# Moving the streamed operands of the matmuls to other start addresses, by pads and column offsets

## The chip, the cores and the metric

The kernel runs on one core of one Trainium2 chip. The metric is the device time of one execution in microseconds. Three runs of the kernel before gave 2610.64, 2612.74 and 2614.07 us; the median, 2612.74 us, is the time before.

## The reference

The model is a backbone of four layers over 256 context tokens and 256 latent tokens of width 1024. Each layer has a token mixer and a squared-ReLU MLP, each behind a modulated RMSNorm and a gated residual. Layers 0 and 3 mix with a bidirectional gated DeltaNet, layer 1 with a short gated convolution, layer 2 with differential attention.

```python
for i in range(DEPTH):
    h_lat = modulate(rmsnorm(x, norm1_g[i]), sh1, sc1)
    h_ctx = modulate(rmsnorm(x_ctx, norm1_g[i]), csh1, csc1)
    y_ctx, y_lat = mixer(h_ctx, h_lat, ...)          # z = h @ w_in; ...; y @ w_out
    x = x + g1 * y_lat
    x = x + g2 * mlp_sqrelu(modulate(rmsnorm(x, norm2_g[i]), sh2, sc2), mlp_w1[i], mlp_w2[i])
    if not last:
        x_ctx = ...                                   # the same for the context tokens
return rmsnorm(x, final_g)

def mlp_sqrelu(h, w1, w2):
    return jnp.square(jax.nn.relu(h @ w1)) @ w2       # 1024 -> 4096 -> 1024
```

All of it is float32. In the last layer only the latent tokens go on after the mixer.

## The kernel before

Activations lie feature-major: 128 features on the partitions, tokens along a row. A full row has TT = 512 columns, 256 context tokens and then 256 latent ones. A large product takes a weight block of 128 x 128 as the stationary operand of TensorE and streams 512 columns (both kinds of token) or 256 (one kind) past it.

To keep float32 accuracy, both operands are split into two parts in the format fp32r, and three matmuls are accumulated for each block (`prod`): weight-high with activation-high, weight-high with activation-low, weight-low with activation-high. The tiles are called `whi` and `wlo` (for the last weights of a stage `whix`, `wlox`) on the weights' side. On the activations' side they are `hh`, `hl` (the normalised input of a mixer or of an MLP), `u` (the squared hidden units of the MLP, high and low under one name in the profile), `y` (the mixer's output in DeltaNet and in attention; in DeltaNet's last heads it lies in tiles called `NT`) and `yh`, `yl` (the mixer's output in the convolution). Each matmul is its own weight load followed by its stream; the load of the next block runs while the present block streams.

Weights come by DMA on SP's queue into three `raw` tiles of 512 KB, ScalarE casts each into `whi`, VectorE (in DeltaNet often GpSimd) makes `wlo`; there are four pairs of `whi` and `wlo`.

A recording layer (`Issue`) takes operations from generators and writes them out by a table of assumed costs. So each engine's order is fixed at build time, and tile pools hand out addresses in the order in which tags are first asked for.

An MLP (`mlp`) takes eight steps. A step makes four blocks of hidden units from `hh`, `hl` (4 blocks x 8 chunks x 3 = 96 matmuls) and then the part of the output that comes from four `u` pairs (8 blocks x 4 x 3 = 96 matmuls). In layers 0 to 2 nearly all have 512 columns; the first step's joint part and the last output rounds are done in halves of 256 (`joint`, `proj_rounds`). In layer 3 the whole MLP has 256 columns, the latent ones, which are the right half of each 512-wide tile.

An address here is the byte offset in a partition, from the built program. The **distance** of a pair of matmuls is the start of the weight block that is being loaded minus the start of the columns that stream at that time, modulo 512. For example: `whi` starts at 54144 and `hh0` at 87680, so the distance is -33536 mod 512 = 256. All weight blocks of 128 columns start at 384 mod 512 (the `x` ones at 256), so the distance depends on the streamed tile alone.

Of the kernel before, what the change touches and what calls it, by code (L numbers as in the profile page):

```python
# [10 lines left out]
F32 = mybir.dt.float32  # L11
# [363 lines left out]
class Net:  # L375
# [3 lines left out]
    MM = 3  # L379
    HP, DHP = -20, -20  # L380
    SHARE = 0.7
    RAW = 3
    RINGS = (dict(u=4, kt=2, E=2, qd=1, NT=2, scr=2, Z=3, gate=2, o=3, NY=1),
             dict(u=4, kt=3, E=3, qd=3, NT=3, scr=3, Z=4, gate=4, o=4, NY=1))

    def __init__(self, tc, ctx, a, depth=4):
        self.tc, self.nc, self.ctx, self.a, self.depth = tc, tc.nc, ctx, a, depth
        self.I = Issue(tc.nc)
        pool = lambda name, bufs, **k: ctx.enter_context(tc.tile_pool(name=name, bufs=bufs, **k))
        self.cp = pool("cp", 1)  # L390
        self.wp = pool("wp", 1)
        self.sp = pool("sp", 1)
        self.psp = pool("psp", 1, space=PSUM)
        self.wlist, self.wt, self.wsplit, self.wraw, self.wdone = [], {}, 0, 0, -1
        self.whome, self.wheld, self.wpool = [], deque(), None
        self.mods = {}
        self.spare_dve = 0
        self.joined = False
        self.wide = True

    def const(self, name, shape, dt=F32):
        return self.I.tile(self.cp, name, shape, dt)
# [304 lines left out]
    def norm_strand(self, i, which, st, half, h):  # L707

        I = self.I
        yield from self.norm_rs(st, half)  # L710
        rs, r, c = st["rs"][half], 1 - half, HALF[half]
        if "A" not in st:
            st["A"] = I.tile(self.sp, f"gain{which}", [P, NCH, 2])
            st["Ak"] = set()
        A = st["A"]
        late = None
        for k in range(NCH):
            q = 12 * which + k // 2
            evs = [self.ada_ev[i][q], self.ada_ev[i][q + 4]]
            if late and not all(e.on for e in evs):  # L720
                yield I.stt(*late)
                I.rel(late[1])
                late = None
            yield evs + [self.tmp_slot(half)]
            mod = self.mods[i]
            if k // 2 not in st["Ak"]:
                st["Ak"].add(k // 2)
                yield from self.gain(i, which, A, k - k % 2)
            tmp = self.norm_tmp(half)
            yield I.stt(tmp, self.x[k][:, c], A[:, k, r:r + 1], rs, ALU.mult, ALU.mult)  # L730
            B = mod[:, 24 * which + k, r:r + 1]
            yield I.act(h[0][k][:, c], tmp, AF.Identity, bias=B)
            if late:
                yield I.stt(*late)
                I.rel(late[1])
            late = (h[1][k][:, c], tmp, B, h[0][k][:, c].bitcast(F32), ALU.add, ALU.subtract)
        yield I.stt(*late)
        I.rel(late[1])
        st["hev"][half].on = True

    def norm_start(self, i, which, st, halves=(0, 1)):
        I = self.I
        h = ([], [])
        for k in range(NCH):
            h[0].append(I.tile(self.sp, f"hh{k}", [P, TT], F32R))
            h[1].append(I.tile(self.sp, f"hl{k}", [P, TT], F32R))
        st["hev"] = [Event(), Event()]
        st["h"] = h
        for half in halves:
            I.spawn(self.norm_strand(i, which, st, half, h), 3 + half)  # L750


    def prod(self, ps, ah, al, bh, bl, first, last):
# [5 lines left out]
    def block(self, wn, rhs, kc, cols, ps, s=slice(0, P), m=P, off=0):  # L759


        c = slice(cols.start - off, cols.stop - off)
        yield [self.have(wn)]
        wh, wl = self.wt[wn]
        for k in range(kc):
            yield [wh, wl, rhs[0][k][:, c], rhs[1][k][:, c]]
            yield from self.prod(ps[0:m, cols], wh[:, k, s], wl[:, k, s], rhs[0][k][:, c], rhs[1][k][:, c], k == 0, k == kc - 1)

    def joint(self, wns, rhs, parts=HALF):


        group = []
        self.wide = False
        for n, wn in enumerate(wns):
            yield [self.mm_slot() if n >= len(wns) - self.MM else self.ch_slot()]
            group.append((wn, self.mm_ps() if n >= len(wns) - self.MM else self.ch_ps()))
        self.wide = True
        for c in parts:
            for k in range(NCH - self.LATE if c is parts[-1] else NCH):
                for wn, ps in group:  # L780
                    yield from self.joint_prod(wn, ps, rhs, c, k)
        return group, rhs, parts[-1]

    def joint_prod(self, wn, ps, rhs, c, k):
        yield [self.have(wn)]
        wh, wl = self.wt[wn]
        m = wh.shape[-1]
        yield [wh, wl, rhs[0][k][:, c], rhs[1][k][:, c]]
        yield from self.prod(ps[0:m, c], wh[:, k, :], wl[:, k, :], rhs[0][k][:, c], rhs[1][k][:, c], k == 0, k == NCH - 1)

    def joint_end(self, group, rhs, c, fin):

        for n, (wn, ps) in enumerate(group):
            for k in range(NCH - self.LATE, NCH):
                yield from self.joint_prod(wn, ps, rhs, c, k)
            self.done(wn)
            fin(n, ps)
            self.joined = n < len(group) - 1
# [53 lines left out]
    def mlp(self, i, t0, st, nst, pl):  # L852
        I = self.I
        halves = [h for h in range(2) if h * T >= t0]
        cols = self.full(t0)
        h = st["h"]
        first = yield from self.joint(pl[0, 0], h, [HALF[x] for x in halves])
        with self.tc.tile_pool(name=f"mlp{i}", bufs=1) as up:
            us = {}
            self.wpool = up  # L860
            ada = Event(i + 1 == self.depth)
            if not ada.on:
                I.spawn(self.ada_rows(i + 1, up, ada), 5000)

            def u_tiles(f):
                us[f] = tuple([I.tile(up, f"u{x}{m}", [P, TT], F32R, 2) for m in range(4)] for x in range(2))

            def u_fin(f, m, ps):
                yield [lambda: I.slot(up, "r", 2)]
                r = I.tile(up, "r", [P, TT], F32, 2, True)  # L870
                u = I.tile(up, "u", [P, TT], F32, 2, True)
                yield I.act(r[:, cols], ps[:, cols], AF.Relu)
                I.rel(ps)
                yield I.act(us[f][0][m][:, cols], r[:, cols], AF.Square)
                yield I.act(u[:, cols], r[:, cols], AF.Square)
                yield I.vtt(us[f][1][m][:, cols], u[:, cols], us[f][0][m][:, cols].bitcast(F32), ALU.subtract)
                I.rel(r, u)

            nf = FF // 512
            for f in range(nf):  # L880
                u_tiles(f)
                if f == 0:
                    yield from self.joint_end(*first, lambda m, ps: I.spawn(u_fin(0, m, ps), 2))
                for m in range(0 if f else 4, 4):
                    yield [self.mm_slot()]
                    ps = self.mm_ps()
                    yield from self.block(pl[0, f][m], h, NCH, cols, ps)
                    self.done(pl[0, f][m])
                    I.spawn(u_fin(f, m, ps), 2)
                if f:  # L890
                    yield from self.proj_rounds(i, pl[1, f - 1], 4, 2, us.pop(f - 1), t0, 40, None)
            if i + 1 < self.depth:
                self.norm_start(i + 1, 0, nst)
            yield from self.proj_rounds(i, pl[1, nf - 1], 4, 2, us.pop(nf - 1), t0, 40, nst)
            self.wpool = None
            yield [ada]

# [90 lines left out]
    def gdn_mixer(self, i, j, last, st, nst, pl):  # L988
# [6 lines left out]
        with self.tc.tile_pool(name=f"gd{i}", bufs=1) as gp:  # L995
# [15 lines left out]
            for step, s in enumerate(self.ORDER[j]):  # L1011
# [27 lines left out]
                else:  # L1039
# [1 line left out]
                    final = heads[-1] == H - 1  # L1041
                    yield [self.y_ev[m] for m in heads]
                    if final:
                        self.norm_start(i, 1, nst, (1,) if t0 else (0, 1))
                    y = [sum((list(self.y[m // 2][x]) for m in heads[::2]), []) for x in range(2)]
                    yield from self.proj_rounds(i, pl[s], len(y[0]), 8 // len(y[0]), y, t0, 16, nst if final else None, t0)
                    self.round_done[n].on = True
# [275 lines left out]
    def gated(self, n, o):  # L1323
# [8 lines left out]
        if last:  # L1332

            yield [self.made[H - 1], self.free("NT", 2)] if 3 not in self.y else []
            if 3 not in self.y:
                y = [self.take("NT", [P, 2, TT], F32R) for x in range(2)]
                self.y[3] = [[y[x][:, m, :TT - t0] for m in range(2)] for x in range(2)]
        elif n // 2 not in self.y:
            self.y[n // 2] = tuple([I.tile(self.gp, f"y{x}{m}", [P, TT - t0], F32R, self.NY) for m in range(2)] for x in range(2))
        yh, yl = self.y[n // 2]  # L1340
        yield from self.split_into(yh[n % 2], yl[n % 2], o)
# [207 lines left out]
    def diff_head(self, n, qk, evs):  # L1549
# [37 lines left out]
        yield I.stt(sq, po, self.gl, sq, ALU.mult, ALU.mult)  # L1587
        I.rel(po)
        if n // 4 not in self.y:
            self.y[n // 4] = tuple([I.tile(dp, f"y{x}{m}", [P, TT], F32R, self.NYD) for m in range(4)] for x in range(2))  # L1590
        yh, yl = self.y[n // 4]
        yield from self.split_into(yh[n % 4], yl[n % 4], sq)
# [194 lines left out]
```

## Time and profile before

| | |
|---|---|
| median of three runs | 2612.74 us |
| the profiled execution | 2613.07 us, with a span of 2611.4 us from first to last instruction |
| TensorE busy | 2515.1 us, 96% of the span |
| VectorE, ScalarE, GpSimd busy | 1899.4, 1257.6, 389.3 us |
| granted TensorE clock, mean | 0.987 |

Matmuls are pipelined, and the profile gives one a duration that reaches past the start of the next. So a matmul's price in a dense stream is the spacing from start to start, which is read from a window's length and the number of matmuls in it, and not the mean duration. Where a stretch has several lines of work, a window over one tile's matmuls counts those alone; a matmul that began just before the window is counted too.

### The profile page before, as it was taken

To read this page: it belongs to the slowest core of one execution; us is meant where nothing else is said; L and a number is where in the kernel's file an instruction comes from. 1 tells how busy PE (TensorE), PEld (TensorE's weight loads), DVE (VectorE), ACT (ScalarE), POOL (GpSimd) and SP (SyncE) were. 2 spreads that over 40 slices of the span, in tenths; PEclk is the share of its full clock that TensorE was granted. 3 is DMA by queue.
4 is the path that set the end of the run, shared out by engine and by line. 5 is a ranking of instruction groups with operands and counts; after the bars stand their busy time and mean duration, and the time that the engine had idled before them with its cause. 6 is when DMAs were issued, how large, how long until landed. Compare 5 with 4: busy or idle time off the path is not lost. (4 is left out here: it accounts for less than half of the span.)

```text
span 2611.4 us, 41997 instructions
## 1 busy us (share of the span) xinstructions
PE 2515.1 (96%) x16396; PEld 2091.5 (80%) x16396; DVE 1899.4 (73%) x3499; ACT 1257.6 (48%) x2343; POOL 389.3 (15%) x273
## 2 busy tenths in 40 slices
PE   6999999899999999999999999999999999997998
PEld 3677777788888988888889666888888878786998
DVE  5776677699975645899856767799965787776665
ACT  4565565543333423533343544543333677765554
POOL 0444444200000000000000000000000254454000
PEclk9999999999999999999999999999999999998999
DMA  6312212456544133565532222365633111122564
GB/s 264 119 50 73 90 50 74 154 189 213 196 144 129 59 97 104 187 210 200 169 115 77 64 73 66 114 213 199 210 124 111 49 50 50 50 58 81 163 185 130
DMA packets 91638, 323.30 MB, mean 124 GB/s; under 512 B 10288, under 2 KB 13872, under 8 KB 91056
## 3 DMA queue, kind: packets, MB, share of 16 engines
q1 hardware_dynamic: 91440, 320.62, 37.8%
q8 instruction: 129, 2.11, 0.3%
q14 instruction: 69, 0.57, 0.1%
HBM read 317.44 MB, written 1.05 MB: 122 GB/s over the span
## 5 line engine op out<-in xcount | busy, mean ns | idle before, releaser
L241 ACT CAST whi<-raw 128x1024 fp32r<-128x1024 f32 x380 | 399.0, 1050 | 799.7 <-PE ch L221 431.9
L254 DVE TENSOR_TENSOR wlo<-raw,whi 128x1024 fp32r<-128x1024 f32 x305 | 374.2, 1227 | 236.6 <-ACT whi L241 236.3
L221 PE MATMUL mm<-hh,whi 128*128 128x512 f32 (+1 forms) x1344 | 490.2, 365 | 1.8 <-DVE x L257 1.1
L221 PE MATMUL mm<-hh,wlo 128*128 128x512 f32 (+1 forms) x1344 | 489.9, 364 | 0.8 <-DVE wlo L254 0.8
L221 PE MATMUL mm<-hl,whi 128*128 128x512 f32 (+1 forms) x1344 | 488.7, 364 | 0.0
L261 DVE CUSTOM_DVE_ANT_0 adaj<-adat,adas,pack 128x1024 bf16<-128x1024 f32 x288 | 368.5, 1280 | 8.5 <-ACT adas L237 5.7
L221 PE MATMUL ch<-hl,whi 128*128 128x512 f32 (+3 forms) x784 | 281.8, 359 | 5.9 <-DVE hl L257 5.9
L221 PE MATMUL ch<-u,whi 128*128 128x512 f32 (+1 forms) x1024 | 287.4, 367 | 0.0
L221 PEld LDWEIGHTS mm<-hh,whi 128*128 128x128 f32 x1344 | 257.8, 192 | 34.4 <-issue 7.7
L221 PEld LDWEIGHTS mm<-hh,wlo 128*128 128x128 f32 x1344 | 257.7, 192 | 32.8 <-issue 6.5
L221 PE MATMUL ch<-hh,whi 128*128 128x512 f32 (+3 forms) x784 | 281.5, 359 | 2.1 <-ACT hh L237 2.1
L221 PE MATMUL ch<-hh,wlo 128*128 128x512 f32 (+3 forms) x784 | 282.1, 360 | 0.0
L221 PEld LDWEIGHTS mm<-hl,whi 128*128 128x128 f32 x1344 | 257.8, 192 | 29.4 <-issue 4.7
L280 POOL TENSOR_TENSOR wlo<-raw,whi 128x1024 fp32r<-128x1024 f32 x75 | 182.0, 2429 | 284.5 <-ACT whi L241 279.6
L221 PE MATMUL mm<-u,whi 128*128 128x512 f32 (+1 forms) x768 | 215.6, 367 | 0.0
L221 PEld LDWEIGHTS ch<-u,whi 128*128 128x128 f32 x1024 | 183.6, 188 | 34.8
L221 PEld LDWEIGHTS <-Z 128*128 128x128 f16 x3072 | 141.0, 98 | 86.2 <-issue 50.2
L221 PE MATMUL ch<-u,wlo 128*128 128x512 f32 (+1 forms) x512 | 187.9, 367 | 0.0
L280 POOL TENSOR_TENSOR qk<-qk,rope 128x512 f32<-128x512 f32 x8 | 13.5, 1685 | 1104.2 <-DMA rt<-qk 1100.4
L221 PE MATMUL ch<-Z 128*128 128x64 f16 (+1 forms) x2816 | 173.0, 201 | 4.8 <-DVE Z L248 3.4
L257 DVE SCALAR_TENSOR_TENSOR x<-mm,mod,x 128x256 f32<-128x256 f32 x285 | 129.4, 479 | 63.7 <-PE mm L221 63.7
L251 DVE CAST_PREDICATED Z<-lev,ch 128x256 f16<-128x256 uint8 x384 | 143.2, 426 | 42.5 <-PE ch L221 40.6
(257 smaller groups left out, 4614.5 us busy)
## 6 DMA issues: line engine op xcount, KB each, us to landing
raw<-in_mlp_w SPq DMA_DIRECT2D x256, 512.0 KB, 3.6
adat<-in_ada_wT SPq DMA_DIRECT2D x144, 512.0 KB, 4.5
raw<-in_gdn_w_in SPq DMA_DIRECT2D x64, 512.0 KB, 3.7
adaw<-in_ada_w SPq DMA_DIRECT2D x48, 512.0 KB, 4.9
raw<-in_sconv_w_in SPq DMA_DIRECT2D x24, 512.0 KB, 3.6
raw<-in_diff_w_in SPq DMA_DIRECT2D x24, 512.0 KB, 3.7
raw<-in_gdn_w_out SPq DMA_DIRECT2D x16, 512.0 KB, 3.6
raw<-in_sconv_w_out SPq DMA_DIRECT2D x8, 512.0 KB, 3.5
```

Of the source, the lines that this page charges most:

```text
L221: op = Op("PE", c, [out], [lhsT, rhs], lambda: self.nc.tensor.matmul(out, lhsT=lhsT, rhs=rhs, start=start, stop=stop, **k), LAT["PE"])
L241: lambda: self.nc.scalar.copy(out=out, in_=in_), LAT["ACT"])
L251: return self.vec(self._n(data), 68, [out], [data], lambda: self.nc.vector.copy_predicated(out=out, mask=mask, data=data))
L254: return self.vec(self._n(in0), 68, [out], [in0, in1], lambda: self.nc.vector.tensor_tensor(out=out, in0=in0, in1=in1, op=op))
L257: return self.vec(self._n(in0), 130, [out], [in0, in1, scalar], lambda: self.nc.vector.scalar_tensor_tensor(out=out, in0=in0, scalar=scala ...
L261: return self.vec(self._n(in0), 130, [out, junk], [in0, in1, init], lambda: self.nc.vector.tensor_tensor_reduce(out=junk, in0=in0, in1=in1 ...
L280: lambda: self.nc.gpsimd.tensor_tensor(out=out, in0=in0, in1=in1, op=op))
```

## The change

Tiles are moved; nothing else is. A dummy tile of 8 columns x n (32 n bytes) is put ahead of some tiles in their pools: 128 bytes at the head of what follows `hh` and `hl` (so all later tiles in the pools, `u` and `yh`, `yl` among them, move by 128 bytes), 352 or 288 bytes ahead of DeltaNet's `y`, and 160 bytes ahead of the attention's `y`. In the last layer's MLP, `hh`, `hl` and `u` no longer keep the latent columns in the right half of their tiles but from column 48 on (`T - SHIFT` = 208 columns lower); the last `y` of that layer (`NT`) starts 48 columns later.

```diff
+    SHIFT = 48
...
+    def pad(self, pool, n):
+
+        self.I.tile(pool, "pad", [P, 8 * n])
...
-        rs, r, c = st["rs"][half], 1 - half, HALF[half]
+        rs, r, c, ch = st["rs"][half], 1 - half, HALF[half], self.cut(HALF[half], st["off"])
...
-            yield I.act(h[0][k][:, c], tmp, AF.Identity, bias=B)
+            yield I.act(h[0][k][:, ch], tmp, AF.Identity, bias=B)
...
-            late = (h[1][k][:, c], tmp, B, h[0][k][:, c].bitcast(F32), ALU.add, ALU.subtract)
+            late = (h[1][k][:, ch], tmp, B, h[0][k][:, ch].bitcast(F32), ALU.add, ALU.subtract)
...
-    def norm_start(self, i, which, st, halves=(0, 1)):
+    def norm_start(self, i, which, st, halves=(0, 1), off=0):
         I = self.I
+        st["off"] = off
...
+        if i == 0 and which == 0:
+            self.pad(self.sp, 4)
...
+    @staticmethod
+    def cut(c, off):
+        return slice(c.start - off, c.stop - off)
...
-                yield I.act(us[f][0][m][:, cols], r[:, cols], AF.Square)
+                yield I.act(us[f][0][m][:, ucols], r[:, cols], AF.Square)
                 yield I.act(u[:, cols], r[:, cols], AF.Square)
-                yield I.vtt(us[f][1][m][:, cols], u[:, cols], us[f][0][m][:, cols].bitcast(F32), ALU.subtract)
+                yield I.vtt(us[f][1][m][:, ucols], u[:, cols], us[f][0][m][:, ucols].bitcast(F32), ALU.subtract)
...
-                        self.norm_start(i, 1, nst, (1,) if t0 else (0, 1))
+                        self.norm_start(i, 1, nst, (1,) if t0 else (0, 1), T - self.SHIFT if t0 else 0)
...
-                self.y[3] = [[y[x][:, m, :TT - t0] for m in range(2)] for x in range(2)]
+                s = self.SHIFT if t0 else 0
+                self.y[3] = [[y[x][:, m, s:s + TT - t0] for m in range(2)] for x in range(2)]
         elif n // 2 not in self.y:
+            if not self.y:
+                self.pad(self.gp, 9 if t0 else 11)
...
+            if not self.y:
+                self.pad(dp, 5)
             self.y[n // 4] = tuple([I.tile(dp, f"y{x}{m}", [P, TT], F32R, self.NYD) for m in range(4)] for x in range(2))
```

The remaining lines hand `off` from `joint`, `joint_prod`, `joint_end`, `mlp` and `proj_rounds` to the operands' column ranges. The built programs have the same instructions in the same order on every engine, with the same waits; only addresses differ. The distances that follow from the two programs, for pairs of fp32r matmuls with 128 weight columns:

| streamed operand, place | columns | pairs | distance before | distance after |
|---|---|---|---|---|
| `hh`, `hl`, layers 0 to 3 | 512 | 3652 | 256 | 256 |
| `u`, MLPs of layers 0 to 2 | 512 | 2013 | 128 | 0 |
| `yh`, `yl`, layer 1 | 512 | 95 | 128 | 0 |
| `y`, layer 2 | 512 | 85 | 288 | 0 |
| `y`, layer 0 | 512 | 73 | 480 | 0 |
| `hh`, `hl`, ahead of the last MLP | 256 | 1354 | 256 | 256 |
| `u` (`whix`), layers 0 to 2; `yh`, `yl` (`whix`), layer 1 | 256 | 760 | 0 | 0 |
| `y`, layer 2 | 256 | 191 | 288 | 0 |
| `y` and `NT`, layer 0 | 256 | 94 and 93 | 480 and 128 | 0 |
| `y` and `NT`, layer 3 | 256 | 124 and 47 | 480 and 128 | 64 and 320 |
| `hh`, `hl`, last MLP | 256 | 768 | 256 | 64 |
| `u`, last MLP | 256 | 671 | 128 | 320 |
| `u` (`whix`), last MLP | 256 | 96 | 0 | 320 |

Apart from these, some 1300 smaller matmuls in layers 0, 2 and 3 (float32, float16, bfloat16) get another distance, because their constants stay where they were while the pools behind them move by 128 bytes.

## Rows read from the trace of the kernel before

**Rows 1.** The page: the span, and TensorE's busy time, share and instructions.

```profile
span 2611.4 us, 41997 instructions
PE 2515.1 (96%) x16396; PEld 2091.5 (80%) x16396; DVE 1899.4 (73%) x3499; ACT 1257.6 (48%) x2343; POOL 389.3 (15%) x273
```

**Rows 2.** Windows inside the MLPs of layers 0 to 3: busy us by engine.

```profile
core 0: us, PE busy (x) PEld busy (x) DVE busy (x) ACT busy (x) POOL busy (x), PEclk, DMA share, GB/s
535.00:840.00 305.00, 305.00 (x1328) 249.00 (x1327) 248.95 (x384) 111.72 (x150) 0.00 (x0) 1.00 0.54 180
1072.00:1380.00 308.00, 308.00 (x1341) 251.47 (x1340) 249.85 (x386) 114.75 (x155) 0.00 (x0) 1.00 0.55 180
1700.00:2008.00 308.00, 308.00 (x1342) 251.53 (x1342) 249.34 (x386) 114.02 (x155) 0.00 (x0) 1.00 0.54 179
2430.00:2600.00 170.00, 170.00 (x1428) 170.00 (x1426) 109.91 (x158) 92.12 (x154) 0.00 (x0) 1.00 0.57 175
```

**Rows 3.** Waits of ScalarE in 600:830 and 2440:2580: total us, times, longest.

```profile
ACT whi L241 <- PE ch L221: 81.7, 22, 4.6
...
ACT whi L241 <- PE ch L221: 34.6, 26, 1.8
```

**Rows 4.** Windows over TensorE's matmuls with tile u: 512 columns twice, then 256.

```profile
598.06:620.45 22.39, 22.39 (x96) 1.00 0.56 192
1766.13:1788.52 22.39, 22.39 (x96) 1.00 0.56 195
...
2439.82:2451.21 11.39, 11.39 (x96) 1.00 0.70 218
```

**Rows 5.** The same over tile hh: 512 columns, then 256.

```profile
576.29:598.06 21.77, 19.70 (x64) 1.00 0.64 215
...
2451.21:2462.71 11.50, 11.50 (x64) 1.00 0.59 185
```

**Rows 6.** The same over tile hl.

```profile
576.29:598.06 21.77, 12.46 (x32) 1.00 0.64 215
...
2451.21:2462.71 11.50, 9.02 (x32) 1.00 0.59 185
```

**Rows 7.** The same over tile whix, then over wlox: u with 256 columns.

```profile
841.29:854.59 13.30, 13.30 (x74) 1.00 0.14 41
...
841.29:854.59 13.30, 10.32 (x37) 1.00 0.14 41
```

**Rows 8.** Timeline of TensorE, layer 1: start us, us, instruction.

```profile
1009.90 0.42 PE L221 MATMUL ch<-yl,whi 128*128 128x512 f32 x1
...
1024.32 0.41 PE L221 MATMUL ch<-yh,whi 128*128 128x512 f32 x1
1024.56 0.40 PE L221 MATMUL ch<-yl,whi 128*128 128x512 f32 x1
1024.79 0.40 PE L221 MATMUL ch<-yh,wlo 128*128 128x512 f32 x1
1025.03 0.28 PE L221 MATMUL ch<-yh,whix 128*128 128x256 f32 x1
1025.14 0.27 PE L221 MATMUL ch<-yl,whix 128*128 128x256 f32 x1
1025.25 0.28 PE L221 MATMUL ch<-yh,wlox 128*128 128x256 f32 x1
```

**Rows 9.** Timeline of TensorE, layer 2, y with 512 columns: first and last.

```profile
1618.02 0.40 PE L221 MATMUL mm<-y,wlo 128*128 128x512 f32 x1
...
1625.71 0.40 PE L221 MATMUL ch<-y,wlo 128*128 128x512 f32 x1
```

**Rows 10.** Timeline of TensorE, y with 256 columns, layers 2 and 3.

```profile
1650.18 0.28 PE L221 MATMUL ch<-y,wlo 128*128 128x256 f32 x1
...
1662.02 0.28 PE L221 MATMUL mm<-y,whi 128*128 128x256 f32 x1
...
2380.50 0.28 PE L221 MATMUL mm<-y,wlo 128*128 128x256 f32 x1
...
2385.05 0.28 PE L221 MATMUL mm<-y,wlo 128*128 128x256 f32 x1
```

More of the change, by code (lines that the diff above doesn't have):

```diff
@@ L759, in block @@
     def block(self, wn, rhs, kc, cols, ps, s=slice(0, P), m=P, off=0):
-        c = slice(cols.start - off, cols.stop - off)
+        c = self.cut(cols, off)
         yield [self.have(wn)]
@@ L767, in block, with joint @@
             yield from self.prod(ps[0:m, cols], wh[:, k, s], wl[:, k, s], rhs[0][k][:, c], rhs[1][k][:, c], k == 0, k == kc - 1)
-    def joint(self, wns, rhs, parts=HALF):
+    def joint(self, wns, rhs, parts=HALF, off=0):
         group = []
@@ L780, in joint, with joint_prod @@
                 for wn, ps in group:
-                    yield from self.joint_prod(wn, ps, rhs, c, k)
-        return group, rhs, parts[-1]
-    def joint_prod(self, wn, ps, rhs, c, k):
+                    yield from self.joint_prod(wn, ps, rhs, c, k, off)
+        return group, rhs, parts[-1], off
+    def joint_prod(self, wn, ps, rhs, c, k, off):
         yield [self.have(wn)]
@@ L787, in joint_prod, with joint_end @@
         m = wh.shape[-1]
-        yield [wh, wl, rhs[0][k][:, c], rhs[1][k][:, c]]
-        yield from self.prod(ps[0:m, c], wh[:, k, :], wl[:, k, :], rhs[0][k][:, c], rhs[1][k][:, c], k == 0, k == NCH - 1)
-    def joint_end(self, group, rhs, c, fin):
+        xh, xl = (rhs[x][k][:, self.cut(c, off)] for x in range(2))
+        yield [wh, wl, xh, xl]
+        yield from self.prod(ps[0:m, c], wh[:, k, :], wl[:, k, :], xh, xl, k == 0, k == NCH - 1)
+    def joint_end(self, group, rhs, c, off, fin):
         for n, (wn, ps) in enumerate(group):
             for k in range(NCH - self.LATE, NCH):
-                yield from self.joint_prod(wn, ps, rhs, c, k)
+                yield from self.joint_prod(wn, ps, rhs, c, k, off)
             self.done(wn)
@@ L856, in mlp @@
         h = st["h"]
-        first = yield from self.joint(pl[0, 0], h, [HALF[x] for x in halves])
+        off = st["off"]
+        ucols = self.cut(cols, off)
+        first = yield from self.joint(pl[0, 0], h, [HALF[x] for x in halves], off)
         with self.tc.tile_pool(name=f"mlp{i}", bufs=1) as up:
@@ L886, in mlp @@
                     ps = self.mm_ps()
-                    yield from self.block(pl[0, f][m], h, NCH, cols, ps)
+                    yield from self.block(pl[0, f][m], h, NCH, cols, ps, off=off)
                     self.done(pl[0, f][m])
@@ L890, in mlp @@
                 if f:
-                    yield from self.proj_rounds(i, pl[1, f - 1], 4, 2, us.pop(f - 1), t0, 40, None)
+                    yield from self.proj_rounds(i, pl[1, f - 1], 4, 2, us.pop(f - 1), t0, 40, None, off)
             if i + 1 < self.depth:
                 self.norm_start(i + 1, 0, nst)
-            yield from self.proj_rounds(i, pl[1, nf - 1], 4, 2, us.pop(nf - 1), t0, 40, nst)
+            yield from self.proj_rounds(i, pl[1, nf - 1], 4, 2, us.pop(nf - 1), t0, 40, nst, off)
             self.wpool = None
```

## The prediction

> **What bounds the kernel.** I read the page's busy times first. TensorE is busy 96% of the span [rows 1]. [...] The waits confirm the direction: there it is ScalarE that waits for TensorE to give back a weight slot, 81.7 us in 230 us of layer 0 and 34.6 us in 140 us of layer 3 in the largest item alone [rows 3]. So in an MLP the time is the number of matmuls times their spacing. A spacing that shrinks by a nanosecond moves the end by as much, and the other engines have room to follow.
>
> Last I read the spacing itself, by operand, from windows over one tile. In layer 0 the 96 matmuls on `u` take 22.39 us, which is 233.2 ns each, and one block in layer 2 takes the same [rows 4]. The block of 96 on `hh` (64) and `hl` (32) just before takes 21.77 us, 226.8 ns each [rows 5, 6]. Both are 512 columns against 128 weight columns in the same format, at the same clock, with no idle time. [...]
>
> **Is it the distance?** `u` also differs from `h` in its weight tiles, which are 256 columns wide. `yh` and `yl` in layer 1 use weight tiles of 128 columns as `h` does, and have distance 128 as `u` does: the 64 spacings from 1009.90 to 1024.79 us are 232.7 ns each [rows 8]. `y` in layer 2 at distance 288 has 33 spacings in 7.69 us, 233.0 ns [rows 9]. So it goes by distance and not by tile.
>
> With 256 columns the picture is another. Distance 256 (`h` in layer 3): 11.50 us for 96, 119.8 ns [rows 5, 6]. Distance 0 (`u` on `whix`): 13.30 us for 74 + 37 = 111, 119.8 ns [rows 7]. Distance 128 (`u` in layer 3): 11.39 us for 96, 118.6 ns [rows 4]. Distance 288: 100 spacings in 11.84 us, 118.4 ns; distance 480: 39 in 4.55 us, 116.7 ns [rows 10]. The weight loads fill these windows completely (170.00 of 170.00 us in layer 3), where with 512 columns they take 82% [rows 2]: with 256 columns a load is as long as a stream.
>
> **The change part by part.** No instruction, wait or transfer is added, removed or moved, so each term is a number of matmuls times a difference of spacings.
>
> 1. `u` with 512 columns, 128 to 0, 2013 pairs. No row of 512 columns stands at distance 0. The lower bound on the time is the spacing of distance 256, 226.8 ns; the upper one is that nothing is gained or that it gets worse (priced below). I take 226.8, because with 256 columns the distances 0 and 256 give the same 119.8 while the other three give less: whatever repeats along the row seems to repeat every 256 bytes. Gain 2013 x (233.2 - 226.8) = 12.9 us.
> 2. `yh`, `yl`, 95 pairs: 95 x (232.7 - 226.8) = 0.6 us. `y` with 512 columns, 85 + 73 pairs: 158 x (233.0 - 226.8) would be 1.0 us. These come in short pieces between other work, so I take 0.6.
> 3. `y` and `NT` with 256 columns in layers 0 and 2 go to distance 0 and lose: 191 x (119.8 - 118.4) + 94 x (119.8 - 116.7) + 93 x (119.8 - 118.6) = 0.27 + 0.29 + 0.11 = 0.7 us.
> 4. The last layer goes to 64 and 320, which are one place if the period is 256. No row shows it. The nearest rows are 288 (32 past 256), 118.4, and 128, 118.6. The shortest single spacing is 0.11 us [rows 8], so 110 ns is the lower bound. [...] I take 117.9, the mean of the three rows off 0 and 256 (118.4, 118.6, 116.7), which is also nearest the two neighbours. Then `h` gives 768 x (119.8 - 117.9) = 1.46 us, `u` 671 x 0.7 = 0.47, `whix` 96 x 1.9 = 0.18, `NT` 47 x 0.7 = 0.03, and `y` loses 124 x 1.2 = 0.15: together 2.0 us. At 110 ns it would be 7.5 + 5.8 + 0.9 + 0.4 + 0.8 = 15.4 us. [...]
> 5. The 1300 small matmuls: nothing. The cover is the waiting around them, and they are short; if each moved by the 2 ns or so that separates the rows at 256 columns, it would be 2.6 us either way.
>
> The sum is 12.9 + 0.6 + 0.6 - 0.7 + 2.0 = 15.4 us. The profiled execution took 2613.07 us (span 2611.4 and 1.7 around it), 0.3 us above the median of 2612.74. From the execution this gives 2597.7, from the median 2597.3; I say 2597.
>
> What is late next: a step of an MLP shortens from 21.8 + 22.4 = 44.2 us to 43.5, by 1.4%. VectorE at 82% and the DMA at 57% do not become the bound from that, so no new wait comes into the sum.
>
> [...] The rows show two spacings for one shape of matmul, 233.2 and 226.8 ns, at a constant clock and without idle time [rows 4 to 6]. [...]
>
> **The rivals.**
>
> *Main case*, as summed: 2597, its own range 2593 to 2602 by the small terms. Chance 0.45.
>
> *The last layer gains much more.* If at 64 the load and the stream no longer meet at all, the spacings fall toward the 110 ns seen singly. [...] Fully, 13.4 + 15.4 gives 2584; half of that, 2591. Chance 0.22.
>
> *Half the gain.* Distance 0 is better than 128 with 512 columns, but not as good as 256, say 230 ns; or 64 costs a few ns. 2013 x 3.2 + 2.5 = 9 us: 2604. For it: the equality of 0 and 256 is read only where the load sets the pace. Chance 0.13.
>
> *The distance does nothing.* `u` and `y` would be slower than `h` for another reason, or 0 would equal 128. 2612.7, less up to 2 us. Against it stands the row of `yh` with weights of the same layout as `h`. [...] Chance 0.12.
>
> *Distance 0 is the worst place for 512 columns* (the slower side). Load and stream would then start on the same spot of the row together and collide from the first column. With 256 columns 0 is indeed at the upper end of the rows [rows 7]. The price by the longest single spacing, 0.24 us [rows 8]: 2013 x 6.8 + 95 x 7.3 + 158 x 7 = 15.5 us, less 2.0, so 2626. It decides once the spacing at 0 is above 236.4 ns: (5.2 + 2.0) / 2266 = 3.2 ns over today's 233.2. Against it: 256 is just as high with 256 columns, and the lowest with 512. Chance 0.08.
>
> **How the numbers follow.** About 0.2%, 5.2 us, is what a measurement of this kernel can tell from no change, so faster means below 2607.5. Main, more and most of half: 0.80. Nothing, and the rest of half: 0.12. Slower: 0.08. The range for 8 in 10 goes from 2586, which leaves out only the last part of the second case, to 2608, which takes in the half case.
>
> **What the profile after would show.** Windows over `u` in layers 0 to 2: a block of 96 in about 21.8 us instead of 22.39; `h` there unchanged at 21.8. The MLPs of layers 0 to 2 shorter by 4.3 us each, and TensorE still without idle time in them. In the last MLP the blocks of `h` and `u` near 11.3 us; a block near 10.6 would be the second case, one above 11.5 a mistake of sign. `y` in layer 2 with 256 columns at 119.8 ns. VectorE and ScalarE with the same durations. What would make the prediction wrong: a `u` block still at 22.4 us or above (period not 256), or TensorE waiting in an MLP for `wlo` or a `raw` tile.

## The result and the profile after

The changed kernel takes 2589.21 us (median of five executions, 2587.76 to 2589.91), against 2612.74 before. The ratio is 0.991, with a 95% interval of 0.9896 to 0.9925: 23.5 us less. Below, a pair of numbers in brackets behind a ratio is always such an interval, and the time named beside a run is that of the kernel before, measured together with it. The profiled execution took 2588.73 us.

The page's head, which answers to [rows 1]: TensorE's busy time fell by 24.2 us with the same 16396 matmuls, and the span by 24.4 us. VectorE and ScalarE are where they were.

```profile
span 2587.0 us, 41997 instructions
PE 2490.9 (96%) x16396; PEld 2080.0 (80%) x16396; DVE 1898.3 (73%) x3499; ACT 1257.8 (49%) x2343; POOL 390.2 (15%) x273
```

Windows inside the four MLPs of the changed kernel, as in [rows 2]. TensorE is still busy in the whole of each. In the last it now makes 1509 matmuls in 171 us, 113.3 ns each, where it made 1428 in 170 us, 119.0 ns.

```profile
core 0: us, PE busy (x) PEld busy (x) DVE busy (x) ACT busy (x) POOL busy (x), PEclk, DMA share, GB/s
530.00:834.00 304.00, 304.00 (x1343) 251.79 (x1342) 250.77 (x388) 114.56 (x155) 0.00 (x0) 1.00 0.55 183
1066.00:1370.00 304.00, 304.00 (x1343) 251.79 (x1342) 249.42 (x386) 114.73 (x155) 0.00 (x0) 1.00 0.55 183
1689.00:1993.00 304.00, 304.00 (x1343) 251.79 (x1342) 248.82 (x386) 113.94 (x155) 0.00 (x0) 1.00 0.55 182
2404.00:2575.00 171.00, 171.00 (x1509) 171.00 (x1509) 114.22 (x163) 97.18 (x164) 0.00 (x0) 1.00 0.58 176
```

Windows over the matmuls on `u` in the changed kernel, for [rows 4]: the block of 96 takes 21.76 us with 512 columns (226.7 ns each; it was 22.39), and 10.88 with 256 (113.3; it was 11.39).

```profile
core 0: us, PE busy (x), PEclk, DMA share, GB/s
595.15:616.91 21.76, 21.76 (x96) 1.00 0.58 197
1754.32:1776.08 21.76, 21.76 (x96) 1.00 0.60 193
2423.37:2434.25 10.88, 10.88 (x96) 1.00 0.72 223
```

The same over `hh` (64 of a block's 96), for [rows 5]. With 512 columns the block is as it was, 21.76 us; in the last MLP it takes 10.88 instead of 11.50.

```profile
616.91:638.67 21.76, 19.68 (x64) 1.00 0.63 215
2434.25:2445.13 10.88, 10.88 (x64) 1.00 0.71 213
```

Both programs issue the same matmuls in the same order, so a stage can be cut at the same matmul in both. Its time is then the difference of two starts (us):

| | DeltaNet 0 | MLP 0 | conv 1 | MLP 1 | attention 2 | MLP 2 | DeltaNet 3 | MLP 3 |
|---|---|---|---|---|---|---|---|---|
| before | 491.5 | 364.0 | 183.0 | 357.0 | 267.9 | 358.0 | 375.8 | 191.6 |
| after | 488.6 | 361.0 | 183.6 | 352.5 | 267.5 | 353.4 | 376.1 | 182.6 |
| difference | -2.9 | -3.0 | +0.6 | -4.5 | -0.4 | -4.6 | +0.3 | -9.0 |

The border of the first two moves between executions (in two later ones of the changed kernel they took 491.8 to 492.3 and 359.5), so these two are to be read together: -5.9 here, -3.8 and -4.3 there. DeltaNet 3 also varies: it lies between 371.8 and 376.2 us in all traces of this case, and takes 372.9 in the third experiment, where no distance changes.

### The profile page after: what moved, and what is told of

It reads as the page before. It is cut to its first block, busy times and chain, and to the rows that moved or that the text cites. A ratio compares the mean times of both kernels' runs of the same rounds, so it can differ in the third digit from the quotient of the medians.

```text
span 2587.0 us, 41997 instructions
## 1 busy us (share of the span) xinstructions
PE 2490.9 (96%) x16396; PEld 2080.0 (80%) x16396; DVE 1898.3 (73%) x3499; ACT 1257.8 (49%) x2343; POOL 390.2 (15%) x273
## 5 line engine op out<-in xcount | busy, mean ns | idle before, releaser
L254 DVE TENSOR_TENSOR wlo<-raw,whi 128x1024 fp32r<-128x1024 f32 x305 | 373.0, 1224 | 230.1 <-ACT whi L241 215.6
L221 PE MATMUL ch<-u,whi 128*128 128x512 f32 (+1 forms) x1024 | 280.5, 361 | 0.0
L221 PE MATMUL mm<-u,whi 128*128 128x512 f32 (+1 forms) x768 | 210.4, 361 | 0.0
L221 PEld LDWEIGHTS ch<-hl,whi 128*128 128x128 f32 (+1 forms) x784 | 146.3, 187 | 30.3 <-DVE hl L257 7.6
```

The lines of the kernel that those rows point to most:

```text
L221: op = Op("PE", c, [out], [lhsT, rhs], lambda: self.nc.tensor.matmul(out, lhsT=lhsT, rhs=rhs, start=start, stop=stop, **k), LAT["PE"])
L254: return self.vec(self._n(in0), 68, [out], [in0, in1], lambda: self.nc.vector.tensor_tensor(out=out, in0=in0, in1=in1, op=op))
```

## The experiments

**The first pad alone.** It moves everything behind `hh` and `hl` by 128 bytes, `u` among it.

```diff
             h[1].append(I.tile(self.sp, f"hl{k}", [P, TT], F32R))
+        if i == 0 and which == 0:
+            I.tile(self.sp, "pad", [P, 32])
```

> The kernel before with the first pad alone: 128 bytes behind hh and hl, nothing else. u, yh, yl and NT go from distance 128 to 0 (2013 + 95 pairs of 512 columns; in the last MLP 671 pairs of 256 columns), y from 480 to 352 and from 288 to 160. Theory A (what counts is the distance between the weight block that loads and the columns that stream, and 0 acts as 256): u blocks of 96 at 21.8 us, gain 12.9 + 0.6, less 0.9 for the last MLP's u at 120 ns instead of 118.6 and 0.2 for NT: 12.4 us, so about 2600. Rival B (the gain of the whole change comes mostly from the last layer): less than 8 us. Rival C (the tile's own place in the row counts, whatever the weights' place): also about 12 us here; the third run tells it from A.

Measured: 2601.4 us beside 2612.3, ratio 0.996 (0.9945 to 0.9974), 10.9 us less where 12.4 was expected. A block on `u` takes 21.76 us, as in the changed kernel:

```profile
core 0: us, PE busy (x), PEclk, DMA share, GB/s
641.70:663.46 21.76, 21.76 (x96) 1.00 0.60 199
```

MLPs 1 and 2 take 352.5 and 353.4 us, as after. MLP 3 takes 192.6, which is 1.0 longer than before: its `u` went from 118.7 ns at distance 128 to 120.0 at 0, as expected. So this part is the gain of the 512-column layers, less 1.0 us.

**The column offsets of the last MLP alone.** The pads are left out; `h` and `u` are put at distance 64.

```diff
-        if i == 0 and which == 0:
-            self.pad(self.sp, 4)
...
+            def uo(f):
+                return T - 16 if t0 else 0
...
-                yield I.act(us[f][0][m][:, ucols], r[:, cols], AF.Square)
+                yield I.act(us[f][0][m][:, self.cut(cols, uo(f))], r[:, cols], AF.Square)
```

> The kernel before with the last MLP's column offsets alone, no pads: hh and hl at distance 64 (768 pairs), u at 64 (671), u on whix at 448 (96), everything else as before. Theory A: 113.3 ns for all at 64, as the changed kernel's trace shows at 64 and 320: 768 x 6.5 + 671 x 5.3 = 8.5 us, about 2604; with the first run the two parts add up to the whole change within 1.5 us. Rival B: over 14 us. Rival D (DMA or ScalarE become the bound when the last MLP goes faster): under 5 us, with TensorE waiting in the last MLP.

Measured: 2602.51 us beside 2612.3, ratio 0.9963 (0.9949 to 0.9977), 9.8 us less. MLP 3 takes 182.6 us, 9.0 less than before; the other stages are within 0.4 us of before, DeltaNet 0 and MLP 0 together 1.0 above it. A block on `u` there:

```profile
core 0: us, PE busy (x), PEclk, DMA share, GB/s
2460.88:2471.76 10.88, 10.88 (x96) 1.00 0.67 197
```

The two parts make 10.9 + 9.8 = 20.7 us of the 23.5, and the change's interval goes from 19.6 to 27.2 (2612.74 times 0.0075 and 0.0104). So they add within the noise, and the stages say it more sharply: MLPs 1 and 2 are as short with the pad alone as in the changed kernel, and MLP 3 is as short with the offsets alone.

**Weights and activations moved together.** The rival was that the activations' new place counts by itself, or that a pad has some other effect.

```diff
+        self.I.tile(self.wp, "pad", [P, 32])
```

> The kernel before with 128 bytes put ahead of the weights too, so raw, whi, wlo and all activations move together by 128 bytes and no distance between weights and activations changes. Theory A: no change, 2612 to 2614, u blocks of 96 still 22.39 us. Rival C (the tile's own place in the row counts): u starts at 384 modulo 512 as in the changed kernel, so u blocks at 21.8 us and about 12 us gained.

Measured: 2612.11 us, ratio 0.9999 (0.9989 to 1.0008). Each `u` block again takes what it took before:

```profile
core 0: us, PE busy (x), PEclk, DMA share, GB/s
642.09:664.48 22.39, 22.39 (x96) 1.00 0.58 194
```

So 128 bytes more in the tile's own place are worth nothing while its distance from the weights stays.

**A ruler over the distances.** The pads of the change are left out, and the eight `u` sets of each MLP stand at eight different distances; the tiles get 128 columns more. In the last MLP `h` stands at 192. The last weights of MLPs 0 to 2 stay in the common pool. Minus lines are those of the changed kernel, here and elsewhere.

```diff
-    SHIFT = 48
+    SHIFT = 16
...
+            def uo(f):
+                return (T if t0 else 0) - [[32, 28, 24, 20, 16, 12, 8, 28], [4, 0, 124, 120, 116, 112, 108, 20], [104, 100, 80, 64, 48, 30, 18, 8], [24, 20, 16, 12, 8, 120, 112, 104]][i][f]
...
-                us[f] = tuple([I.tile(up, f"u{x}{m}", [P, TT], F32R, 2) for m in range(4)] for x in range(2))
+                us[f] = tuple([I.tile(up, f"u{x}{m}", [P, TT + 128], F32R, 2) for m in range(4)] for x in range(2))
```

> A ruler, not a faster kernel: in the MLPs of layers 0 to 2 each of the eight steps keeps u at another column offset, so one run shows 512 columns at distances 0 to 240 in steps of 16 and at 8, 56, 320, 384, 448, and 256 columns at 16, 48, 96; in the last MLP 256 columns at 32, 48, 64, 80, 96, 160, 192 and, for h, 192. The last weights of the first three MLPs come through the common slots to make room. Theory A with a period of 256: 320, 384, 448 equal 64, 128, 192; 0 at 226.7, 128 at 233.3 (512 columns), 64 at 113.3 and 32 near 118.4 (256 columns). A period of 512 instead: 320, 384 and 448 differ from 64, 128 and 192 by 2 ns or more. [...]

Windows over `u` in this kernel, at distances 0, 64 and 192 with 512 columns, then 32 and 64 with 256:

```profile
core 0: us, PE busy (x), PEclk, DMA share, GB/s
554.10:575.86 21.76, 21.76 (x96) 1.00 0.58 193
730.20:752.60 22.40, 22.36 (x96) 1.00 0.45 148
1318.10:1340.10 22.00, 22.00 (x96) 1.00 0.32 96
2447.00:2458.40 11.40, 11.40 (x96) 1.00 0.77 226
2492.40:2503.30 10.90, 10.90 (x96) 1.00 0.65 194
```

The distances 320, 384 and 448 give the spacings of 64, 128 and 192 (233.3, 233.3 and 229.05 ns), the last two with the same pattern of single spacings: with 512 columns the period is 256 bytes, and distances are given modulo 256 from here on. With 512 columns 0 is the lowest, and 64 gives 233.3. With 256 columns 0 is among the slowest (120.0 ns in the first experiment), and 64 gives the lowest block of this run. So no place measured is the best for both widths.

**The ruler with finer steps.** The same code with other offsets; `h` in the last MLP stands at 112.

```diff
-    SHIFT = 48
+    SHIFT = 36
...
+                return (T if t0 else 0) - [[31, 29, 27, 26, 25, 23, 22, 18], [21, 19, 17, 15, 14, 10, 6, 14], [2, 126, 118, 110, 106, 98, 97, 4], [18, 17, 15, 14, 10, 2, 31, 118]][i][f]
```

> The ruler again, at distances between the first ones: 512 columns at 4, 12, 20, 24, 28, 36, 40, 44, 52, 60, 68, 72, 88, 104, 120, 136, 168, 200, 216, 248, 252; 256 columns at 4, 40, 56, 60, 68, 72, 88, 112, 120. Theory A with sharp places: 512 columns stay at 229 to 235 ns next to 0 (4, 248, 252) as at 8, 256 columns at 116 ns or more next to 64 (60, 68). If instead a good place is some tens of bytes wide, 4, 252, 60 and 68 are within 1 ns of 226.7 and 113.3.

Measured by both rulers on `u`, ns a matmul, each from one block of 96 or 112. With 256 columns some places have a second value, which comes below:

| columns | distance: spacing |
|---|---|
| 512, low | 0, 4, 20: 226.7; 192: 229.05; 36, 68: 230.0; 200: 230.1; 144, 80: 231.1; 52, 176: 231.2 |
| 512, middle | 8, 12, 16, 24, 32, 56, 60, 64, 72, 88, 104, 112, 120, 128, 160, 168, 208, 216, 224, 248: 233 to 233.5; 240: 231.7 |
| 512, high | 96, 136, 40, 48: 234.2 to 234.7; 252: 236.6; 28: 236.7; 44: 238.7 |
| 256 | 64: 113.4; 68: 115.7; 4: 116.7; 16: 117.1; 96: 117.3; 192: 117.8; 32: 118.3; 112: 118.6; 48, 80: 119.1 to 119.3; 160: 119.9; 56, 60, 72, 88: 120.0; 40: 121.3; 120: 122.6 |

A good place has bad ones 4 to 8 bytes away: with 512 columns 252 and 8 around 0, with 256 columns 60 and 72 around 64. That 4 and 20 are as good as 0 with 512 columns was not expected, and nothing here explains it. One rival stays open in the fine steps: both rulers move the stream alone, so distance and the stream's own place change together there. The third experiment parts the two for 128 bytes, and a later one, where the weights are moved by 64 bytes instead, for 64; for steps of 4 to 60 bytes no run does. Two rows of this kernel, distances 20 and 28:

```profile
core 0: us, PE busy (x), PEclk, DMA share, GB/s
640.29:662.06 21.77, 21.77 (x96) 1.00 0.59 199
728.04:750.77 22.73, 22.73 (x96) 1.00 0.45 146
```

**Own block or next block.** 128 bytes between the `whi` and the `wlo` tiles of the kernel before.

```diff
+            if n == 0:
+                I.tile(pool, "pad", [P, 32])
             lo = I.tile(pool, "wlo" + tag, [P, kc, cols], F32R, bufs)
```

> The kernel before with 128 bytes between the whi tiles and the wlo tiles. All tiles behind move along, so the high and the low weight blocks now stand at different distances from one stream: for h with 512 columns a whi block is at 128 and a wlo block at 0 (mod 256), for u with 512 columns a whi block at 0 and a wlo block at 128. The three products of a chunk run in the order whi with high, whi with low, wlo with high. Theory N (a stream is slowed by the load of the block that comes next, which runs while it streams): on u the second spacing of each three (whi with low, while wlo is loaded) is the long one, about 233 ns, and the first and third are 226.7; on h the second is the short one. Theory O (it is the block's own place that counts): on u the third (wlo with high) is long, on h the third is short. By both, if spacings add one by one, 96 on u take 96 x 228.9 = 21.97 us, 96 on h 96 x 231.1 = 22.19 us, and a step of an MLP the same 44.2 us as before, so the whole stays within 2 us of 2612. Theory S (a run settles into one pace that does not decompose into single spacings): the three spacings do not repeat in threes, and blocks take 21.76 or 22.4 us.

Measured: 2617.24 us, one execution beside 2612.05; the expected 2612 was missed. Windows over `u`, where 21.97 was expected:

```profile
core 0: us, PE busy (x), PEclk, DMA share, GB/s
596.02:618.22 22.20, 22.20 (x96) 1.00 0.55 186
640.60:662.79 22.19, 22.19 (x96) 1.00 0.58 196
```

From start to start the spacings do repeat in threes (means over some 670 each on `u`): 227.0 ns where this and the next block are `whi` (both at 0), 232.4 from `whi` to `wlo` (at 128), 234.1 from `wlo` back to `whi`. So theory S falls, but N and O are each only half of it. On `u` a spacing is short only where the stream's own block and the next one both stand at 0, so one misplaced block in three costs two spacings. On `h` the same two spacings are long (232.3 and 234.3), and so is the one between two blocks at 128 (232.6). Hence `h` loses 6.3 ns in all its matmuls (233.1 against 226.8) and `u` gains only 2.0, which is why the stages that go by the matmuls' pace are slower: conv 1, MLP 1 and MLP 2 by 3.7, 2.6 and 3.1 us. DeltaNet 3 and MLP 3 are shorter, by 4.0 and 1.5. Why both places count is not shown.

**The remaining 256-column pairs to 64.** The change leaves `whix` in layers 0 to 2 and attention's second `y` at distance 0, where 256 columns take 119.8 to 120.0 ns; at 64 the last MLP takes 113.3.

```diff
+            if home and home == self.padded:
+                self.pad(pool, 2)
...
+            if self.y:
+                self.pad2(dp, 6)
+            self.y[n // 4] = tuple([I.tile(dp, f"y{n // 4}{x}{m}", [P, TT], F32R) for m in range(4)] for x in range(2))
```

> The changed kernel, and the 256-column pairs that it left at 0 moved to 64 or 320 too, where a pad is enough: 64 bytes ahead of the first whix of layers 0 to 2 (u on whix, 570 pairs; yh, yl on whix, 190), and the attention's second y tiles, which only stream 256 columns, 192 bytes further (191 pairs). Theory A: 951 pairs from 120.0 to 113.3 ns: 6.3 us below the changed kernel, about 2583. Rival E (the ends of those MLPs are bound by the residual and norm work that follows, so a faster stream there only waits): no more than 2 us below it.

> The changed kernel once more, beside the run above on one chip: 2588 to 2590.

> The version with the remaining 256-column pairs moved to 64, again, beside the changed kernel on the same chip. By the stages of the first runs the moved pairs save 3.4 us (0.7 in each of MLPs 0 to 2, 0.3 in the convolution, 1.1 in the attention): about 2586 to 2587 where the changed kernel has 2590. The rival is the difference of the medians of the first runs, 7 us, which would need a gain in the DeltaNet of layer 3 that the edit does not touch; the other rival is no difference (under 1 us).

> The changed kernel again on the same chip: 2589 to 2591 us, ratio 0.991 to 0.992 to the kernel before.

Measured on a first chip: 2584.34 us (ratio 0.9905, 0.989 to 0.992; one of the five executions took 2592.39) beside the changed kernel's 2591.66 (0.9924, 0.9912 to 0.9937), which had been expected at 2588 to 2590. On a second: 2587.07 (0.9908, 0.9894 to 0.9921) beside 2589.58 (0.9921, 0.9907 to 0.9934). The intervals overlap both times. By stages of the profiled executions the moved pairs in conv 1, MLPs 1 and 2 and the attention save 0.3, 0.7, 0.7 and 1.1 us on the first chip, and 0.0, 0.4, 0.3 and 0.8 on the second; the rest of the first difference lies mostly in DeltaNet 3 (372.9 against 375.7), which the edit does not touch and which varies by as much without it. So this version is the lowest measured, by 1.5 to 3 us that the times alone do not settle; the 6.3 us that were hoped for did not come. One reason is seen in its windows over `whix`, both at distance 64 (with `wlox` there are 112 matmuls in the first and 80 in the second):

```profile
core 0: us, PE busy (x), PEclk, DMA share, GB/s
836.98:850.08 13.10, 13.10 (x75) 1.00 0.12 41
850.75:859.70 8.95, 8.95 (x53) 1.00 0.01 2
```

From start to start the first runs at 117.8 ns, the second, behind its first six matmuls, at 113.3. At one distance, in one kernel, there are two paces. On the second chip the second block of MLP 1 ran at 117.8 and those of MLPs 0 and 2 at 113.3, so the place in the program does not fix the pace either. In this kernel the weights were moved to reach 64, and in the last MLP of the change the stream was; both show 113.3 and 117.8, so here too it is the distance that counts.

**The two paces.** The changed kernel has them too: in its first profile the 39 spacings on `y` in DeltaNet 3, at 64, from 2365.11 to 2369.70 us, are 117.8 ns, and all blocks of 96 in the last MLP are at 113.3. Its repeat on the second chip showed this on the largest scale: its five executions took 2588.77, 2589.36, 2589.58, 2595.39 and 2595.94 us. The one of 2595.94, 6.4 over the median, was profiled. Its last MLP took 189.3 us instead of 182.6, which is all of that. A window over `u` there:

```profile
core 0: us, PE busy (x), PEclk, DMA share, GB/s
2447.28:2458.59 11.31, 11.31 (x96) 1.00 0.64 186
```

And a window of all engines inside that MLP:

```profile
core 0: us, PE busy (x) PEld busy (x) DVE busy (x) ACT busy (x) POOL busy (x), PEclk, DMA share, GB/s
2410.00:2575.00 165.00, 165.00 (x1403) 165.00 (x1403) 108.68 (x150) 94.60 (x157) 0.00 (x0) 1.00 0.61 182
```

1403 matmuls in 165 us are 117.6 ns, at the full clock and without idle time; a block of 96 gives 117.8. Two kernels asked what decides it: other distances for `u` between the blocks of `h` at 64, and one such block at the head only.

```diff
+            def uo(f):
+                return T - [0, 80, 96, 120, 88, 124, 104, 48][f] if t0 else 0
...
+                return T - [80, 48, 48, 48, 48, 48, 48, 48][f] if t0 else 0
```

> The changed kernel with other column offsets for u in the last MLP: h stays at 64, and the eight u sets stand at 0, 192, 128, 32, 160, 16, 96 and 64 in turn, so that the stream on h enters distance 64 seven times from a dense stream at the full clock with another distance. In one execution of the changed kernel the whole of this stage ran at 117.8 ns a matmul, in the others at 113.3. Theory A (the pace at 64 is taken up where the stream enters, and stays): the h blocks each have one pace from start to end, 113.3 or 117.8 (10.88 or 11.31 us for 96), and which one can differ from block to block. Theory B (after a dense stream it is always the lower one, the higher one needs the clock's rise or a gap): the seven later h blocks are all at 113.3. Theory C (the pace belongs to the execution, not to the entry): all h blocks alike in the execution, 113.3 or 117.8. The u blocks themselves 120.0, 117.8, 118.6, 118.3, 119.9, 117.1, 117.7 ns as at those distances before.

> The changed kernel with the first of the eight u sets of the last MLP at distance 192 instead of 64, all else there at 64: costs 96 x 4.5 ns = 0.4 us where the stage runs at 113.3. If the pace is taken up at the entry and an entry from a dense stream at 192 gives the lower one, all five executions lie within 2 us of 2590, with none near 2596, where the changed kernel has had two of fifteen. If the entry does not decide, or decides for the higher one, executions near 2596 stay or all of them are there.

Of the first, the windows over `hh` after `u` at 160 and after `u` at 16:

```profile
core 0: us, PE busy (x), PEclk, DMA share, GB/s
2527.20:2538.10 10.90, 10.90 (x64) 1.00 0.67 194
2549.35:2560.66 11.31, 11.31 (x64) 1.00 0.57 185
```

The stream on `h` has a block behind six of the new distances: after 0, 192, 128, 32 and 160 it ran at 113.3 ns, after 16 at 117.8. So both paces occur in one execution, after dense streams at the full clock, and each, once a few matmuls have passed, lasts until the distance changes. That is theory A; B and C fall. The second kernel took 2590.53, 2592.41, 2596.96, 2597.62 and 2597.67 us (median 2596.96, ratio 0.9937, 0.9923 to 0.9952). The profiled one of these (2592.41) has 117.8 ns in the first `u` block, the one at 192, and 113.3 in every later block of 96; that the three near 2597 have 117.8 there too is argued from the 6 us between them. If so, a fixed entry from 192 does not fix the pace. What does was not found.

Nor is 64 the only place with more than one pace. These are blocks with 256 columns at distance 192 (`u` on `whix` in the second experiment, then `hh` in the first ruler) and at 112 (`hh` in the second ruler, twice; `hl` makes up the 96):

```profile
core 0: us, PE busy (x), PEclk, DMA share, GB/s
2580.56:2591.32 10.76, 10.76 (x97) 1.00 0.01 2
...
2503.28:2514.59 11.31, 11.31 (x64) 1.00 0.62 188
...
2524.68:2536.07 11.39, 11.39 (x64) 1.00 0.61 185
2547.59:2558.48 10.89, 10.89 (x64) 1.00 0.65 193
```

At 192 that is 95 spacings of 113.3 ns in one run and 117.8 in every block of another. At 112 five blocks of `h` run at 118.6 to 118.7 and one, behind `u` at 88, at 113.4. So with 256 columns the values in the table are one pace each of places that may have several, and do not rank the places; that 64 is better than 192 or 112 is not shown.

## Why the prediction was right, and where it was off

It said 2597 with 2586 to 2608; the time is 2589.21. The direction, the place and the mechanism (TensorE bounds the MLPs, and the distance sets the spacing there) hold. One term was mis-sized by 7 us, and a small one did not show.

*Term 1, `u` from 128 to 0* (12.9 us): right. The block went from 22.39 to 21.76 us where 21.8 was said, so 2013 x (233.2 - 226.7) = 13.1 us, and MLPs 1 and 2 are shorter by 4.5 and 4.6 us where 4.3 was said. The guess behind it, that the spacing repeats every 256 bytes, was read from the rows at 0 and 256 with 256 columns; the first ruler bears it out with 512 (64 and 320 both give 233.3 ns).

*Term 2, `yh`, `yl` and `y` with 512 columns* (1.2 us): not seen in the time. Their spacing did fall (`y` in layer 2: 33 spacings in 7.52 us, 227.8 ns, against 233.0). But conv 1 took 183.6 us, not less than 183.0. TensorE waits for ScalarE's `yh` ahead of them, 3.2 us here and 3.0 before; the granted clock then falls to half. Windows there in the changed kernel (columns as above) show it at half for 6.8 us:

```profile
998.00:1001.40 3.40, 2.80 (x6) 0.50 0.87 282
1001.40:1004.80 3.40, 3.40 (x10) 0.50 0.77 200
1004.80:1008.20 3.40, 3.40 (x16) 0.99 0.37 139
```

In the kernel before it was at half for 3.4 us:

```profile
1003.00:1006.50 3.50, 0.84 (x2) 1.00 0.79 268
1006.50:1010.00 3.50, 3.50 (x10) 0.51 0.66 181
1010.00:1013.50 3.50, 3.50 (x17) 1.00 0.78 260
```

In the changed kernel nine spacings at half the clock take 3.84 us there (from 1000.42 to 1004.26), 427 ns each; 22 at the full clock take 4.99 us (from 1006.85 to 1011.84), 227 ns each. So 3.4 us more at half, some 8 matmuls, cost 1.6 us by an estimate from these spacings, which is more than the 0.6 that `yh` and `yl` were to give. It is no accident of one execution: all eight traces with `yh` and `yl` at 0 show 6.8 us at half there and a conv 1 of 183.1 to 183.6 us, and all five with them at 128 show 3.4 us and 183.0 to 183.2. Why the longer stretch goes with the move is not shown.

*Term 3, `y` with 256 columns at 0* (a loss of 0.7 us): right where it was read. In layer 2 it is 101 spacings in 12.12 us, 120.0 ns, against 118.4 before and 119.8 foretold.

*Term 4, the last MLP at 64 and 320* (2.0 us): mis-sized. The step that failed is the value taken, 117.9 ns, "the mean of the three rows off 0 and 256". Measured: 113.33 ns, so 768 x 6.5 on `h`, 671 x 5.3 on `u`, 96 x 6.5 on `whix`, together 9.1 us; the stage shows 9.0. A mean of neighbours assumes a smooth course between them. The ruler shows none: 32 gives 118.3, 48 gives 119.1, 60 and 72 give 120.0, and 64 between them 113.4. The 7.1 us missed here are most of the 8 between 2597 and 2589. About half of the second rival's gain (2591) is what came. The block near 10.6 us that was its mark did not: 10.88 is the lowest block of 96 in any run here. The rival's 110 ns was read from rows that are rounded to 10 ns: from start to start those two spacings are 115 and 113 ns. The 117.9 is, by accident, close to the second pace of the same place, and the execution profiled at that pace, 2595.94 us, lies within 2 us of the forecast. That one place can have two spacings, so that the same program can take 2589 or 2596 us, is in no case of the prediction.

*Term 5, the small matmuls* (nothing): DeltaNet 3 and the attention moved by +0.3 and -0.4 us, less than DeltaNet 3 varies by itself.

*With 256 columns a load is as long as a stream*: misread. The weight loads fill the window because their records overlap. A load's record lasts 0.19 us with 512 columns and with 256 (first line, then two), and with 256 the next starts 0.12 us later:

```profile
659.96 0.19 PEld L221 LDWEIGHTS mm<-u,wlo 128*128 128x128 f32 x1
...
2499.86 0.19 PEld L221 LDWEIGHTS ch<-hl,whi 128*128 128x128 f32 x1
2499.98 0.19 PEld L221 LDWEIGHTS ch<-hh,wlo 128*128 128x128 f32 x1
```

So that the load sets the pace with 256 columns, which the rival "half the gain" leans on, is not shown by these rows. No term of the sum rests on it.

*The rivals.* That the distance does nothing falls by the first experiment, and that it is the tile's place and not the distance by the third. Spacings of one shape, 512 columns, run from 226.7 to 238.7 ns by the start addresses alone, at the full clock and without idle time. That with 512 columns 0 is worse than 256, or the worst place of all, falls: both give 226.7 ns, and no place of the rulers is lower. No new wait came, as said: TensorE is busy for the whole of each MLP window, with VectorE at 82.5% of it and the DMA at 58% or less (the 82% and 57% that it went by are read from [rows 2]).

## What to carry to other kernels

Where TensorE is busy without a gap and each matmul loads its own weights, compare the spacing from start to start between operands of one shape at one clock: a difference of a few ns per matmul can be a matter of addresses (here 226.7 against 233.2), and a pad of some bytes is a cheap thing to try. Measure the distances in the kernel itself, with high and low weights alike; do not interpolate. Here distance 0 gave 226.7 ns with 512 columns, the lowest measured, but 120.0 with 256, where 64 gave 113.3; and 252, which is 4 bytes from 0, gave 236.6 ns, more than the 233.2 of the start at 128. Take several blocks and several executions before trusting or ranking a place, because one place can have more than one pace (64 with 256 columns: 113.3 and 117.8 ns).

## What the runs showed of the hardware that was not expected

- The spacing depends on the distance between weight block and stream modulo 256 bytes: 226.7 to 238.7 ns with 512 columns, 113.3 to 122.6 with 256. For steps under 64 bytes the stream's own place was not parted from the distance.
- At distance 64 with 256 columns there are two steady paces, 113.3 and 117.8 ns, each kept over more than 1400 matmuls. Two of fifteen executions of the changed kernel lay at the time that the upper one gives, and one of these, profiled, had it. At 192 blocks ran at 113.3 and at 117.8 ns, at 112 at 113.4 and at 118.7.
- The places of a stream's own weight block and of the next one both count: with every third block 128 bytes off, the spacings on `u` were 227.0, 232.4 and 234.1 ns.
- Why the distance counts, why 4 and 20 are as good as 0 with 512 columns, and what picks the pace at 64 stay open. Most other distances were seen in one execution only, so a second pace at them is not excluded.
